# Two decoder layers on one core: order of the float32 products, of the readers of the column sums, of the sines, and one last store

## The chip, the cores and the metric

The kernel runs on one core of a Trainium2 chip. The metric is the device time of one execution in microseconds (us), lower is better. The time before is the median of three runs, 876.67 us (876.50 to 876.76).

## What is computed

A trunk of two layers on 256 tokens of width 1024, all in float32, then a last RMSNorm. The part that matters here is the first half of a layer:

```python
h = rmsnorm(x, norm_mix)
proj = h @ w_in                      # 8192 columns: cb, cc, cu, q, k, v, g, ga, gb
y_conv = short_conv_mixer(cb, cc, cu, conv_w, w_conv_out)
# retention: 4 heads, q and k rotated by cos/sin of the positions
scores = einsum(q, k) * decay        # 128 x 128 within a chunk; 2 chunks
o = scores @ v + what the state of the first chunk gives
o = (o - mean(o)) * rsqrt(var(o) + EPS) * ret_norm
y_ret = (silu(g) * o) @ w_ret_out
x = x + (sigmoid(ga) * y_conv + sigmoid(gb) * y_ret) @ w_o
x = x + square(relu(rmsnorm(x, norm_mlp) @ w_up)) @ w_down
```

`rmsnorm` and the norm of `o` are worked out as one over a square root of column sums; the sums come from products with a matrix of ones, so they stand in PSUM.

## The kernel before, in words

Every weight is cut into blocks of 1024 x 256 (512 KB in two halves); there are 152. `window(products)` (L153) is the unit of the program: one call per block. The call number `i` runs the work that `at(n, fn, ph=...)` (L132) had queued for it, in phases -1, 0, 1, 2, splits block `i + 2` between the phases, issues the products of block `i` on TensorE, and asks SP for block `i + 3`. The order on each engine is the order of these calls; no scheduler changes it.

To split (`split`, L104; `split_half`, L148) means that ACT casts a half block (128x1024) to a rounded part (L105) and DVE subtracts it from the half (L106), so that TensorE multiplies rounded and rest in `float32r`. `proj` (L183) multiplies one block: 16 pairs of a product with 512 columns and one with 256, the 256 one with the part that DVE made. The first pair of a block therefore waits for ACT, and its second product for DVE. After a block the sums in PSUM are collected: ACT copies one part (L234), DVE adds the other (L235).

The places that the change touches:

- `rsqrt_begin` (L244) reads column sums `v` from PSUM twice: ACT takes the root (L246), DVE the scaled mean plus EPS (L247). It is called from `factors_begin` (L408; first norm of each layer, 128x256, in window 6 of layer 0) and from `head_roots` (L582; twice per layer, 128x512, for the variances of two heads each; at 158 and 168 us in layer 0, 585 and 595 us in layer 1). The two Newton steps on the root (`newton`, L238) are in later windows: ACT squares (L240), DVE multiplies twice (L241, L242).
- `sines` (L388), in layer 0 alone: three ACT functions (L391 to L393) with a table of their own, at the end of window 5. `rotation_tables` (L395) on POOL makes `sin_t` and `cos_t` from them (L397 to L401) in window 6. `rotations` (L422, DVE, L424) uses them in window 8.
- `scores` (L541): per head three `float32r` products of 256 columns (`three`, L537), then one full float32 product of 128 columns (TensorE runs it as two records) for the second chunk. `mix_values` (L554): the same for the values, two groups per head, where the float32 product adds into half of the columns of the group.
- the end (L842 to L848): DVE scales the last 512 columns of the second 128 tokens in two pieces, SP stores each (L819); ACT scales and stores the other 512 columns.

Of the kernel before, what the change touches and what calls it, by code (L numbers as in the profile page):

```python
# [16 lines left out]
ALU = mybir.AluOpType  # L17

P = 128
D = 1024  # L20
T = 256
# [4 lines left out]
EPS = 1e-6  # L26
# [27 lines left out]
def trunk_kernel(ctx, tc, px, pos, w, mask, gf, out):  # L54
    nc = tc.nc
# [28 lines left out]
    def stile(name):  # L84
        return s8.tile([P, KT, T], F32, tag="s8", name=name)

    class Parts:
# [5 lines left out]
        def at(self, k):  # L93
            return self.tiles[k // (KT // 2)][:, k % (KT // 2)]
# [34 lines left out]
    work, small_products, amid = {}, {}, {}  # L129
# [50 lines left out]
    def mm(o, a, b, start, stop):  # L180
        nc.tensor.matmul(o, lhsT=a, rhs=b, start=start, stop=stop, skip_group_check=True)  # L181

    def proj(act, n_blocks=1):  # L183

        ps = ps_main.tile([P, 2, 2, T], F32, tag="mm", name="ps")

        def products(blk, b):  # L190
            for k in range(KT):
                a = act[b].at(k)
                for j in range(2):
                    first, end = b == 0 and k == 0, b == n_blocks - 1 and k == KT - 1
                    mm(ps[:, j], blk[:, 0, 2 * k + j, :], a, first, False)
                    mm(ps[:, j, 1], blk[:, 1, 2 * k + j, :], a[:, 0], False, end)
                    for fn, args in amid.pop((cnt[0], 2 * k + j), []):
                        fn(*args)

        for b in range(n_blocks):  # L200
            window(lambda blk: products(blk, b))
        return ps
# [40 lines left out]

    def rsqrt_begin(y, m, v, scale):  # L244

        nc.scalar.activation(y, v, AF.Abs_reciprocal_sqrt, scale=scale, bias=eps)  # L246
        nc.vector.tensor_scalar(out=m, in0=v, scalar1=scale, scalar2=EPS, op0=ALU.mult, op1=ALU.add)  # L247

    def column_sums(o, hi, lo):

# [87 lines left out]
    for n in range(2):  # L338
        c = slice(4 * n, 4 * n + 4)
# [9 lines left out]
    def first_parts(norm=norm):  # L349

        def parts(i, *ks):
            for n, k in enumerate(ks):
                norm.split(k)
                split_half(i, n)

        at(0, parts, 1, 2, 3)
        at(1, parts, 2, 4, 5)
        at(2, parts, 3, 6, 7)
        at(3, norm.split, 0)
        for i, half in ((4, 0), (4, 1)):  # L360
            at(3, split_half, i, half)
        for p in range(NPAIR):
            at(3 if p < 3 else 4, norm.square, p)
        at(4, norm.fold)
        at(5, norm.split_sum)
# [37 lines left out]
    for layer in range(DEPTH):  # L403
# [4 lines left out]
        def factors_begin(norm=norm):  # L408
            rs_m, rs_a = (tmp.tile([P, T], F32, tag="tmp1", bufs=7, name=n) for n in ("rs_m", "rs_a"))
            rsqrt_begin(rr, rs_m, norm.total_ps, 1.0 / D)  # L410
            at(1, newton, rr, rs_a, rs_m, ph=-1)
            at(2, factors_end, rs_m, rs_a, ph=-1)
# [17 lines left out]
        if layer == 0:  # L430
            first_parts()
            at(0, reduce_angles)
            at(5, sines, ph=2)
            at(6, rotation_tables)
            at(9, nc.sync.dma_start, mask_sb, mask)
        if layer == 0:
            products_at(5, norm_total)
# [5 lines left out]
        v1 = s4.tile([P, HEADS, T], F32, tag="s4", name="v1")  # L443
        qk = q_parts = k0_parts = sg = ta = tb = None
        yc, yr = None, Parts("yr", 0)
        sc0_parts = sc1 = None
# [87 lines left out]
            nc.gpsimd.tensor_tensor(out=acc, in0=y, in1=acc, op=ALU.mult)  # L534
            at(1, split, acc, *yc.pair(p))

        def three(o, a, b, stop):  # L537
            for n, (i, j) in enumerate(((0, 0), (0, 1), (1, 0))):
                mm(o, a[i], b[j], n == 0, stop and n == 2)

        def scores(h):  # L541
            ps = ps_misc.tile([P, T + P], F32, tag="misc", name="sc_ps")
            q, k = qk[:, h, P:], qk[:, HEADS + h, P:]
            three(ps[:, :T], [k0_parts[:, i, h, :] for i in range(2)], [q_parts[:, i, h, :] for i in range(2)], True)
            mm(ps[:, T:], k, q, True, True)
            at(1, weigh_scores, h, ps)

        def weigh_scores(h, ps):
# [5 lines left out]
        def mix_values(h):  # L554
            ps = ps_misc.tile([P, 2, T], F32, tag="misc", name="o_ps")
            for j in range(2):
                c = slice(j * P, (j + 1) * P)
                three(
                    ps[:, j, :], [v0_parts[:, i, h, c] for i in range(2)],
                    [sc0_parts[:, i, h, :] for i in range(2)], False,  # L560
                )
                mm(ps[:, j, P:], v1[:, h, c], sc1[:, h, :], False, True)
            at(1, gate_values, h, ps)

        def gate_values(h, ps):
# [16 lines left out]
        def head_roots(i, st):  # L582

            if i == 0:
                new("rm", s8.tile([P, 2, HEADS, T], F32, tag="s8", name="rm"))
            rm = kept["rm"]
            h = slice(2 * i, 2 * i + 2)
            rs = rm[:, 0, h, :]
            rsqrt_begin(rs, rm[:, 1, h, :], st, 1.0 / T)
            later = 2 + i  # L590
            for n in range(2):
                at(later + n, lambda: newton(rs, t2("rs_a"), rm[:, 1, h, :]))
            for n in range(2):
                at(later + 1 + n, head_out, 2 * i + n, rs[:, n, :])
# [17 lines left out]
        for name, _ in IN_ORDER:  # L612
            n = seen[name] = seen.get(name, -1) + 1
            if name == "q" and n == 0:
                qk = stile("qk")
                q_parts = s8.tile([P, 2, HEADS, T], F32R, tag="s8", name="q_parts")
                k0_parts = s4.tile([P, 2, HEADS, P], F32R, tag="s4", name="k0_parts")
            elif name == "cc" and n == 0:
                yc = Parts("yc")
            elif name == "cc" and n == 2:  # L620
                sc0_parts = s8.tile([P, 2, HEADS, T], F32R, tag="s8", name="sc0_parts")
                sc1 = s4.tile([P, HEADS, P], F32, tag="s2", bufs=1, name="sc1")
                for h in range(HEADS):
                    products_at(1 + h, scores, h)
            elif name == "g" and n == 2:
                osq = s8.tile([P, 2, HEADS, T], F32R, tag="s8", name="osq")
                for h, later in enumerate((0, 0, 1, 2)):
                    products_at(later, mix_values, h)
                products_at(2, head_sums, 0)
                products_at(4, head_sums, 1)  # L630
            elif name == "ga" and n == 0:
                ta = stile("ta")
            elif name == "gb" and n == 0:
                tb = stile("tb")
            ps = proj(act)
# [112 lines left out]
    o = stile("o").rearrange("p k t -> p (k t)")  # L748
    o = [o[:, j * D:(j + 1) * D] for j in range(2)]
# [9 lines left out]
    ps = [[both_ps[:, c] for c in HALVES], [third[:, HALVES[0]], ps_misc.tile([P, 512], F32, tag="misc", name="ps")]]  # L759
# [37 lines left out]
    def root(j):  # L797

        rest, part = sums[j][:, 0:1], sums[j][:, 1:2]
        m, r, a = (small.tile([P, 1], F32, tag=f"{n}{j}", bufs=1, name=n) for n in ("fin_m", "fin_r", "fin_a"))  # L800
        nc.scalar.activation(r, part, AF.Sqrt, bias=rest)
        nc.vector.tensor_tensor(out=m, in0=part, in1=rest, op=ALU.add)
        nc.vector.reciprocal(r, r)
        nc.vector.scalar_tensor_tensor(out=a, in0=r, scalar=m, in1=r, op0=ALU.mult, op1=ALU.mult)
        nc.vector.scalar_tensor_tensor(out=r, in0=a, scalar=3.0, in1=r, op0=ALU.subtract, op1=ALU.mult)
        return r
# [6 lines left out]
    def scaled(j, n, c, r):  # L813

        f = slice(512 * n + c.start, 512 * n + c.stop)
        nc.vector.scalar_tensor_tensor(
            out=o[j][:, f], in0=ps[j][n][:, c], scalar=r, in1=gain[:, f], op0=ALU.mult, op1=ALU.mult
        )
        nc.sync.dma_start(out=out[tok[j], f], in_=o[j][:, f])  # L819
# [19 lines left out]
    c = HALVES[0]  # L839
# [2 lines left out]
    nc.vector.tensor_tensor(out=o[1][:, c], in0=ps[1][0], in1=gain[:, c], op=ALU.mult)  # L842
    squares(1, 1)
    r = root(1)
    for n in range(2):
        scaled(1, 1, slice(256 * n, 256 * n + 256), r)
    nc.scalar.activation(o[1][:, c], o[1][:, c], AF.Copy, scale=r)
    nc.scalar.dma_start(out=out[tok[1], c], in_=o[1][:, c])  # L848

# [73 lines left out]
```

## Time and profile before

| | |
|---|---|
| median of 3 runs | 876.67 us |
| the profiled execution's own time | 876.84 us |
| its span | 875.0 us, 12663 instructions |
| TensorE products busy | 866.8 us, 99% |
| weight loads on TensorE busy | 754.1 us, 86% |
| DVE busy | 680.2 us, 78% |
| ACT busy | 529.5 us, 61% |
| POOL busy | 308.4 us, 35% |
| granted TensorE clock | full, 0.999 in the mean |
| HBM read | 161.66 MB, 186 GB/s |

The profile page gives the busy share of each engine and a chain of waits; the views of the trace give each instruction with its start, its length and, in brackets, how long its engine had been idle and what ended that. TensorE is busy nearly all the time, so the end moves only where TensorE waits, where its work gets longer or shorter, or behind its last product.

### The profile page before, as it was taken

What the parts mean: (1) busy time and instruction counts of PE and PEld (TensorE: products, weight loads), DVE (VectorE), ACT (ScalarE), POOL (GpSimd) and SP (SyncE); (2) the same over time, 40 slices, a digit from 0 to 9 for tenths busy, and PEclk for the clock granted to TensorE, in tenths of its full rate; (3) what the DMA queues carried; (4) which work ended last, traced back from release to release, by engine and by line L of the source; (5) the groups of instructions that cost most, each with busy time, mean ns of one, the idle gap of its engine ahead of it and who ended that gap; (6) DMA issues with size and microseconds to landing.
All of it is one profiled execution on the core that took longest, in us unless ns stands there. A gap on an engine that the chain in (4) does not pass through costs nothing.

```text
span 875.0 us, 12663 instructions
## 1 busy us (share of the span) xinstructions
PE 866.8 (99%) x4846; PEld 754.1 (86%) x4846; DVE 680.2 (78%) x739; ACT 529.5 (61%) x761; POOL 308.4 (35%) x191
## 2 busy tenths in 40 slices
PE   9999999999999999999999999999999999999997
PEld 6888888888888888888888888888888888888885
DVE  5799899999898766555567989999979896663443
ACT  6766665956467777444447665578645587772333
POOL 3857755361213222000013587455411322240000
PEclk9999999999999999999999999999999999999999
DMA  9746455556655655555554555545565565565541
GB/s 329 231 170 208 138 194 183 168 174 226 202 194 170 216 187 193 196 188 187 178 199 167 183 172 195 171 158 187 185 210 175 194 198 189 191 218 171 196 137 48
DMA packets 45996, 163.53 MB, mean 187 GB/s; under 512 B 5104, under 2 KB 5744, under 8 KB 45936
## 3 DMA queue, kind: packets, MB, share of 16 engines
q1 hardware_dynamic: 45648, 162.29, 55.4%
q8 instruction: 38, 0.62, 0.3%
q10 hardware_dynamic: 288, 0.44, 0.2%
q14 instruction: 22, 0.18, 0.1%
HBM read 161.66 MB, written 1.05 MB: 186 GB/s over the span
## 4 chain that ended last, share of the span: by engine, by line
PE 87%; POOL 5%; DVE 4%; DMA 1%; ACT 1%; issue 1%; SPq 0%; DVEq 0%; POOLq 0%
PE ps L181 85%; DVE parts L106 2%; PE o_ps L181 1%; DMA pos_i<-pos 1%; POOL red L371 1%; POOL ang L386 1%; DMA raw<-w 1%; POOL mix_sum L281 1%; POOL rot L458 1%; POOL qk L459 0%; DVE sum L235 0%; PE sc_ps L181 0%; ACT parts L105 0%; POOL qk L451 0%; POOL acc L534 0%
## 5 line engine op out<-in xcount | busy, mean ns | idle before, releaser
L106 DVE TENSOR_TENSOR parts<-raw,parts 128x1024 fp32r<-128x1024 f32 (+1 forms) x304 | 436.7, 1474 | 94.2 <-ACT parts L105 93.8
L105 ACT CAST parts<-raw 128x1024 fp32r<-128x1024 f32 (+1 forms) x304 | 304.5, 1049 | 110.8 <-PE ps L181 79.8
L181 PE MATMUL ps<-mix,parts 128*128 128x512 f32 (+1 forms) x1792 | 316.1, 337 | 1.0 <-DVE parts L106 1.0
L181 PEld LDWEIGHTS ps<-mix,parts 128*128 128x128 f32 x1792 | 274.0, 188 | 38.9 <-DVE parts L106 1.6
L181 PE MATMUL ps<-mlp,parts 128*128 128x512 f32 (+1 forms) x1024 | 178.1, 336 | 0.0
L181 PEld LDWEIGHTS ps<-mlp,parts 128*128 128x128 f32 x1024 | 156.5, 188 | 20.9
L730 POOL TENSOR_TENSOR u<-u,rr2m 128x512 f32<-128x512 f32 x32 | 46.5, 1454 | 126.2 <-ACT u L729 113.1
L235 DVE TENSOR_TENSOR sum<-ps,sum 128x512 f32<-128x512 f32 x78 | 53.3, 684 | 47.4 <-ACT sum L234 47.3
L181 PE MATMUL ps<-up,parts 128*128 128x512 f32 (+1 forms) x512 | 88.9, 336 | 0.0
L181 PE MATMUL ps<-parts,up 128*128 128x512 f32 x384 | 87.5, 389 | 0.0
L181 PEld LDWEIGHTS ps<-up,parts 128*128 128x128 f32 x512 | 78.3, 188 | 10.5
L181 PEld LDWEIGHTS ps<-parts,up 128*128 128x128 f32 x384 | 71.9, 188 | 14.9
L234 ACT COPY sum<-ps 128x512 f32<-128x512 f32 x78 | 45.4, 583 | 61.9 <-PE ps L181 61.7
L181 PE MATMUL ps<-yr,parts 128*128 128x512 f32 (+1 forms) x256 | 44.7, 336 | 0.0
L181 PE MATMUL ps<-mg,parts 128*128 128x512 f32 (+1 forms) x256 | 44.7, 336 | 0.0
L181 PE MATMUL ps<-yc,parts 128*128 128x512 f32 (+1 forms) x256 | 44.7, 336 | 0.0
L181 PEld LDWEIGHTS ps<-yc,parts 128*128 128x128 f32 x256 | 39.1, 188 | 5.2
L181 PEld LDWEIGHTS ps<-yr,parts 128*128 128x128 f32 x256 | 39.1, 188 | 5.2
L181 PEld LDWEIGHTS ps<-mg,parts 128*128 128x128 f32 x256 | 39.1, 188 | 5.2
L181 PE MATMUL ps<-parts,mix 128*128 128x512 f32 x180 | 41.6, 392 | 0.0
L181 PEld LDWEIGHTS ps<-parts,mix 128*128 128x128 f32 x180 | 33.7, 188 | 7.5 <-ACT parts L105 0.6
L281 POOL TENSOR_TENSOR mix_sum<-mix_sum,sq 128x512 f32<-128x512 f32 x6 | 9.9, 1644 | 83.4 <-ACT sq L279 83.2
(166 smaller groups left out, 747.5 us busy)
## 6 DMA issues: line engine op xcount, KB each, us to landing
raw<-w SPq DMA_DIRECT2D x302, 512.0 KB, 4.0
raw<-w SPq DMA_DIRECT2D x4, 256.0 KB, 5.0
px_sb<-px SPq DMA_DIRECT2D x3, 256.0 KB, 7.3
mask_sb<-mask SPq DMA_DIRECT2D x1, 512.0 KB, 7.6
gain<-gf SPq DMA_DIRECT2D x1, 512.0 KB, 4.5
out<-o SPq DMA_DIRECT2D x2, 256.0 KB, 2.1
out<-o SPq DMA_DIRECT2D x2, 128.0 KB, 2.0
out<-o ACTq DMA_DIRECT2D x1, 256.0 KB, 2.2
```

The lines of the kernel that those rows point to most:

```text
L105: nc.scalar.copy(hi, src)
L106: nc.vector.tensor_tensor(out=lo, in0=src, in1=hi.bitcast(F32), op=ALU.subtract)
L181: nc.tensor.matmul(o, lhsT=a, rhs=b, start=start, stop=stop, skip_group_check=True)
L234: nc.scalar.copy(t, ps[:, :, 1, :])
L235: nc.vector.tensor_tensor(out=t, in0=ps[:, :, 0, :], in1=t, op=ALU.add)
L281: nc.gpsimd.tensor_tensor(out=self.sum, in0=self.sum, in1=sq, op=ALU.add)
L371: nc.gpsimd.tensor_scalar(out=out, in0=x_, scalar1=c0, op0=ALU.mult, **ops)
L386: nc.gpsimd.tensor_tensor(out=ang, in0=ang, in1=red, op=ALU.subtract)
L458: nc.gpsimd.tensor_tensor(out=w_, in0=w_, in1=both(sinr), op=ALU.mult)
L730: nc.gpsimd.tensor_tensor(out=u, in0=u, in1=both(rr2), op=ALU.mult)
```

## The change

Four edits. The mean on DVE is written ahead of the root on ACT in `rsqrt_begin`; the sines and the rotation tables go one window later; the float32 product goes to the first place in `scores` and to the second in each group of `mix_values`; the last two pieces of the output become one piece and one store.

```diff
     def rsqrt_begin(y, m, v, scale):
 
+        nc.vector.tensor_scalar(out=m, in0=v, scalar1=scale, scalar2=EPS, op0=ALU.mult, op1=ALU.add)
         nc.scalar.activation(y, v, AF.Abs_reciprocal_sqrt, scale=scale, bias=eps)
-        nc.vector.tensor_scalar(out=m, in0=v, scalar1=scale, scalar2=EPS, op0=ALU.mult, op1=ALU.add)
...
             at(0, reduce_angles)
-            at(5, sines, ph=2)
-            at(6, rotation_tables)
+            at(6, sines, ph=2)
+            at(7, rotation_tables)
...
-        def three(o, a, b, stop):
+        def three(o, a, b, amid=lambda: None):
+
             for n, (i, j) in enumerate(((0, 0), (0, 1), (1, 0))):
-                mm(o, a[i], b[j], n == 0, stop and n == 2)
+                mm(o, a[i], b[j], n == 0, n == 2)
+                if n == 0:
+                    amid()
...
-            three(ps[:, :T], [k0_parts[:, i, h, :] for i in range(2)], [q_parts[:, i, h, :] for i in range(2)], True)
             mm(ps[:, T:], k, q, True, True)
+            three(ps[:, :T], [k0_parts[:, i, h, :] for i in range(2)], [q_parts[:, i, h, :] for i in range(2)])
...
-                    [sc0_parts[:, i, h, :] for i in range(2)], False,
+                    [sc0_parts[:, i, h, :] for i in range(2)],
+                    lambda: mm(ps[:, j, P:], v1[:, h, c], sc1[:, h, :], False, False),
                 )
-                mm(ps[:, j, P:], v1[:, h, c], sc1[:, h, :], False, True)
...
-    for n in range(2):
-        scaled(1, 1, slice(256 * n, 256 * n + 256), r)
+    scaled(1, 1, c, r)
```

On ACT, in windows 5 to 7 of layer 0, the piece of the difference (a + is the changed kernel; `rr` is the root, `mix_st` the column sums, `sh` and `turns` the sines, `parts` the halves of the weight blocks, `sg` a collected gate):

```order
 L105 CAST parts<-raw 128x1024
+L247 ACT_TABLE_LOAD
+L247 ACTIVATE rr<-mix_st,eps 128x256
+L481 ACTIVATE v_parts<-vt,mu 128x256 x2
+L234 COPY sg<-ps 128x512
+L105 CAST parts<-raw 128x1024 x2
 L391 ACT_TABLE_LOAD
 L391 ACTIVATE sh<-ang 128x256
 L392 ACTIVATE turns<-ang 128x256
 L393 ACTIVATE turns<-turns,quarter_turn 128x256
-L246 ACT_TABLE_LOAD
-L246 ACTIVATE rr<-mix_st,eps 128x256
```

The root and the two casts of window 6 now stand ahead of the sines; the number of table loads is the same.

At the first `head_roots` of layer 0, before: ACT (first four rows, `rm` is the root, `var_ps` the sums) and DVE (last four), with the semaphores that each row waits for:

```order
L567 ACTIVATE osq<-o_ps 128x512 [waits DVE_49,PE_49]
L246 ACT_TABLE_LOAD
L246 ACTIVATE rm<-var_ps,eps 128x512 [waits PE_49]
L234 COPY ta<-ps 128x512
...
L570 SCALAR_TENSOR_TENSOR sg<-o_ps,hg,sg 128x256
L247 TENSOR_SCALAR rm<-var_ps 128x512 [waits Activation_49]
L235 TENSOR_TENSOR ta<-ps,ta 128x512 [waits Activation_49]
L106 TENSOR_TENSOR parts<-raw,parts 128x1024 [waits DMAHW7_49,Activation_49]
```

The same place in the changed kernel:

```order
L570 ACTIVATE osq<-o_ps 128x512 [waits DVE_49,PE_49]
L247 ACT_TABLE_LOAD
L247 ACTIVATE rm<-var_ps,eps 128x512 [waits DVE_49]
L234 COPY ta<-ps 128x512
...
L573 SCALAR_TENSOR_TENSOR sg<-o_ps,hg,sg 128x256
L246 TENSOR_SCALAR rm<-var_ps 128x512 [waits PE_49]
L235 TENSOR_TENSOR ta<-ps,ta 128x512 [waits Activation_49]
L106 TENSOR_TENSOR parts<-raw,parts 128x1024 [waits DMAHW7_49,Activation_49]
```

No instruction changes its place on its engine here; the wait between the two readers of the sums turns round: before, DVE waits for ACT's root, now ACT's root waits for DVE.

## Rows read from the trace of the kernel before

**Rows 1.** Timeline of TensorE's weight loads: start us, us, engine, what [idle before <-releaser]
```profile
95.59 0.19 PEld L181 LDWEIGHTS ps<-mix,parts 128*128 128x128 f32 x1 [0.95 <-DVE parts L106]
...
107.89 0.19 PEld L181 LDWEIGHTS ps<-mix,parts 128*128 128x128 f32 x1 [0.66 <-DVE parts L106]
```

**Rows 2.** Busy time by window: window, its us, busy us of each engine, clock, DMA
```profile
46.50:78.80 32.30, 32.30 (x188) 28.49 (x187) 32.04 (x33) 20.43 (x30) 18.65 (x11) 1.00 0.57 194
...
156.50:214.90 58.40, 58.40 (x338) 51.46 (x338) 57.80 (x56) 42.58 (x57) 24.52 (x13) 1.00 0.58 190
```

**Rows 3.** Timeline of DVE around the first norm of layer 0
```profile
40.01 1.23 DVE L106 TENSOR_TENSOR parts<-raw,parts 128x1024 fp32r<-128x1024 f32 x1 [0.21 <-ACT parts L105]
44.38 0.42 DVE L247 TENSOR_SCALAR rs_m<-mix_st 128x256 f32<-128x256 f32 x1 [3.14 <-ACT rr L246]
...
46.59 2.58 DVE L106 TENSOR_TENSOR parts<-raw,parts 128x1024 fp32r<-128x1024 f32 x2 [0.19 <-ACT parts L105]
...
50.48 2.35 DVE L106 TENSOR_TENSOR parts<-raw,parts 128x1024 fp32r<-128x1024 f32 x2
52.74 0.42 DVE L241 SCALAR_TENSOR_TENSOR rs_a<-rs_a,rs_m 128x256 f32<-128x256 f32 x1
```

**Rows 4.** Timeline of ACT in the same stretch
```profile
39.99 1.28 ACT L391 ACT_TABLE_LOAD   x1
...
43.87 0.47 ACT L246 ACTIVATE rr<-mix_st,eps 128x256 f32<-128x256 f32 x1
...
47.41 0.41 ACT L240 ACTIVATE rs_a<-rr 128x256 f32<-128x256 f32 x1
```

**Rows 5.** Timeline of POOL, and of DVE beside it, in the same stretch
```profile
42.64 0.74 POOL L397 TENSOR_TENSOR sin_t<-sh,turns 128x256 f32<-128x256 f32 x1 [3.26 <-ACT turns L393]
...
44.37 0.61 POOL L400 TENSOR_TENSOR cos_t<-sh 128x256 f32<-128x256 f32 x1
...
46.58 1.96 POOL L482 TENSOR_SCALAR v<-vt,mu 128x256 f32<-128x256 f32 x1
...
47.75 1.41 DVE L106 TENSOR_TENSOR parts<-raw,parts 128x1024 fp32r<-128x1024 f32 x1
```

**Rows 6.** Timelines of ACT and DVE at the head roots of layer 0
```profile
158.05 0.69 ACT L246 ACTIVATE rm<-var_ps,eps 128x512 f32<-128x512 f32 x1
...
159.10 1.06 ACT L105 CAST parts<-raw 128x1024 fp32r<-128x1024 f32 x1
...
168.09 0.69 ACT L246 ACTIVATE rm<-var_ps,eps 128x512 f32<-128x512 f32 x1
...
159.06 0.68 DVE L247 TENSOR_SCALAR rm<-var_ps 128x512 f32<-128x512 f32 x1
...
160.26 1.21 DVE L106 TENSOR_TENSOR parts<-raw,parts 128x1024 fp32r<-128x1024 f32 x1
...
169.49 0.69 DVE L247 TENSOR_SCALAR rm<-var_ps 128x512 f32<-128x512 f32 x1
```

**Rows 7.** Timelines of DVE and TensorE at the third block of `yc`
```profile
199.98 1.21 DVE L106 TENSOR_TENSOR parts<-raw,parts 128x1024 fp32r<-128x1024 f32 x1
...
204.07 0.51 PE L181 MATMUL ps<-yc,parts 128*128 128x512 f32 x2
```

**Rows 8.** Chain of waits in order of time, layer 0: start us, us, what
```profile
113.48 0.57 PE sc_ps L181 x5
...
137.41 2.31 PE o_ps L181 x20
```

**Rows 9.** Timeline of the end, and the table of DMA issues (last number: us to landing)
```profile
870.88 0.88 DVE L816 SCALAR_TENSOR_TENSOR o<-ps,fin_r,gain 128x256 f32<-128x256 f32 x2
871.39 0.81 SPq L819 DMA_DIRECT2D out<-o  x2
871.63 0.35 ACTq L848 DMA_DIRECT2D out<-o  x1
...
out<-o ACTq DMA_DIRECT2D x1, 256.0 KB, 2.2
```

## The prediction

> **What bounds the kernel now.** I looked at the page's busy shares first: TensorE is at work 99% of the span at full clock. So a microsecond saved on DVE, ACT or POOL counts only if TensorE waited for it, and the reader should look for TensorE's waits next. After the first 10 us, which the change leaves alone, there are two, both in layer 0 and both for the part of a block that DVE makes: 0.95 and 0.66 us, 1.6 us together [rows 1]. They are the end of a backlog: from 46.5 to 78.8 us DVE is busy 32.04 of 32.30 us [rows 2], and behind that the chain goes over POOL, which DVE releases, to the same blocks. A second stretch matters where TensorE does not wait: from 156.5 to 214.9 us DVE is busy 57.80 of 58.40 us [rows 2], so whatever delays it there is not made up before 215 us. The tightest block in it is the third of `yc`: DVE ends its half at 199.98 + 1.21 = 201.19, TensorE starts the block at 204.07 and wants that half for its second product, some 0.2 us on [rows 7]. The reserve is about 3.1 us. Behind the last product there are only the last norm and the stores.
>
> **Float32 products: 0.** Nothing is added; 8 products for scores and 16 for values change places. A group of three `float32r` products and one float32 product takes 0.57 us in the scores, where a 512-column product follows, and 2.31 / 4 = 0.58 in the values, where mostly a 256-column product follows [rows 8]. What stands behind the float32 product thus makes 0.01 us. Every neighbour it gets is of a kind it had somewhere before (a 256-column product ahead, a 256- or 512-column one behind). Taking 0.01 us either way for 24 products bounds the edit at -0.2 to +0.2 us; I take 0. Its earlier wait for POOL or DVE is covered too: its operands are made ahead of the split parts that the other three products of its group need.
>
> **First norm of layer 0: the root, the sines, the tables.** Before, ACT ran the sines first, from 39.99, and the root began at 43.87 [rows 4]; DVE sat idle 3.14 us until then, because its mean waited for ACT's root [rows 3]. Now:
>
> - DVE takes the mean right behind the half that ends at 40.01 + 1.23 = 41.24, so it ends at 41.7. ACT has its table by 39.99 + 1.28 = 41.27 and must wait for the mean: the root starts at 41.7, 2.2 us earlier. The mean costs ACT 0.4 us here.
> - From root to first Newton square ACT took 47.41 - 43.87 = 3.54. Now the sines lie between: 43.87 - 39.99 less one load of 1.28, so 2.60. The square starts at 41.7 + 3.54 + 2.60 = 47.84 and ends at 48.25, 0.4 later than before.
> - DVE's two halves, which ended at 46.59 + 2.58 = 49.17 [rows 3], end 2.2 earlier, at 47.0. The Newton step behind them now waits for ACT's square until 48.25, 0.9 us ahead of the old 49.17. To the second Newton step at 52.74 it is 3.6 us of DVE's own work. Undisturbed, DVE is there at 51.85: 0.9 ahead.
> - It isn't undisturbed. The tables on POOL, from 42.64 on [rows 5], ran while DVE was idle. Now they start at 47.8, beside DVE's work. The first, 0.74, overlaps the first Newton step by some 0.3; the other two-input step, 0.61, falls on a half of a block, and I charge 0.25; the scalar steps I charge at 0.15, since a half beside such a step took 1.41 instead of 1.21 [rows 5, 7]. Together 0.7.
>
> So DVE comes 0.2 us earlier out of window 7, and TensorE's two waits shrink by 0.2 together. Between bounds of 0.9 (POOL costs nothing) and -0.3 (worked out under the third rival) I choose by those rows. The ceiling is the 1.6 us of waits.
>
> The Trainium skill, page "SBUF — State Buffer", section "Who interferes with whom", has a harder rule: a VectorE instruction with two inputs in SBUF and a GpSimd instruction that reads SBUF shut each other out for the whole instruction. By it this term would be a loss of 0.3 us, the lower bound above, instead of a gain of 0.2. The row here is milder: the half at 47.75 went on beside a scalar step that lasted until 48.54, and lost only 0.2.
>
> **Head roots, both layers: what the turned wait costs.** This is the edit's hidden price. In `head_roots` ACT used to be ahead: its root ran at 158.05, and DVE, deep in its queue, read the sums at 159.06 and had not waited. Now the root waits for the mean, until 159.06 + 0.68 = 159.74: ACT and everything behind it (the collecting copy, both casts) is 1.7 us later. DVE waits for these in turn. From root to the end of the first cast ACT takes 159.10 + 1.06 - 158.05 = 2.11, so DVE's next half can start 2.1 us behind the mean instead of 160.26 - 159.74 = 0.5 [rows 6]: 1.6 us lost. The second pair has the same order (168.09 against 169.49, [rows 6]), so it loses 1.6 again. DVE is 3.2 us late from 171 us on, against a reserve of 3.1: TensorE waits 0.1. Bounds: 0, if DVE makes something up, to 2.3, if POOL, released during DVE's waits, gets in ahead of a half at each pair, at 1.1 a time (what a second half loses beside POOL's 512-column steps is of the size of a half, 1.21). Layer 1 repeats it, but there nothing waits in the rows, and I charge 0. In the first norm of layer 1 DVE has no backlog, so the turned wait costs nothing.
>
> **Last store: -0.3.** Two pieces of 256 columns take DVE from 870.88 to 871.76, and SP issues the second store until 871.39 + 0.81 = 872.20. One piece of 512 columns out of PSUM should take about 0.7 (the 512-column mean in [rows 6] took 0.68), so the store is issued from 871.6, at the time of ACT's own (871.63), and lands at the same time [rows 9]. ACT's lands 2.2 later, at 873.8; the second piece's issue started near 871.8, at the end of a queue of three, and at 2.2 lands at 874.0 or a little later. Bounds 0 (the larger store takes longer by what it starts earlier) to -0.4; I take -0.3.
>
> **Sum.** 0 - 0.2 + 0.1 - 0.3 = -0.4 us on the profiled execution's 876.84, which stands 0.17 above the median of 876.67. On the median that is 876.3.
>
> **Rivals.**
>
> - Faster: POOL's tables cost DVE nothing and the two orders of POOL and DVE fall well, so that the chain comes 0.9 to 1.6 us early and TensorE's waits go. For it: ACT's new order frees 2.2 us. Against it: the Newton square itself is 0.4 late. With the store that is 876.67 - 0.9 - 0.3 = 875.5 down to 874.8. Chance 0.14.
> - Slower: the turned wait in `head_roots`. For it: DVE's full stretch [rows 2], which gives nothing back. It decides the time once DVE's delay passes 3.1 us; at 5.4 (2 x 1.6 and 2 x 1.1) TensorE waits 2.3 in layer 0, and the time is 876.67 + 2.3 - 0.3 = 878.7; at half of that, 877.5. Against it: the order of POOL and DVE has to fall badly twice. Chance 0.12.
> - Nothing: POOL's steps shut DVE out for their whole length. Then the second half of the Newton step waits out the whole scalar step of the tables, some 0.5 us more than charged, the front loses 0.3 and the store gains 0.3: 876.67 + 0.3 + 0.1 - 0.3 = 876.8. Chance 0.12. (This is the rule of the Trainium skill named above.)
>
> **How the numbers follow.** The forecast, 876.3, has the chance that is left, 0.62; its own bounds are about 875.4 to 877.2. The range goes to 875.1 on the faster side and to 877.5 on the slower, and leaves out the far half of either rival. About 0.2% of this time, 1.75 us, is what a measurement can tell from no change. Faster by more than that needs 874.9: only the far end of the first rival, 0.07. Slower needs 878.4: the far part of the second, 0.06. The rest, 0.87, is the same.
>
> **What would show it.** Right: on ACT the root of the first norm starts near 41.7 and the sines behind 45; DVE's idle time of 3.14 us is split into smaller ones, one of them ended by ACT's square; TensorE's two waits add up to 1.2 to 1.6 us. At the head roots ACT's root starts right behind DVE's mean, with idle time of 1.5 to 2 us on ACT and about 1.3 us on DVE ahead of its collecting add, twice per layer; the reserve at the third block of `yc` is near nothing. SP has one store at the end, near 871.6 on the old scale. The float32 groups stay at 0.57 to 0.58. Wrong: TensorE's waits gone, or new waits of over 0.5 us between 170 and 215 us, or float32 groups that differ by more than 0.02 us.

## The result, and the profile after

The changed kernel takes 882.11 us (median of 4 runs, 880.0 to 883.52) where the kernel before took 876.67 in the same session (876.5 to 876.76). The ratio is 1.0056, with a 95% interval of 1.0041 to 1.0072: 5 us **slower**, and far more scattered. The forecast was 876.3, with a range up to 877.5. The profiled execution took 881.02 us, 4.18 more than the profiled one before.

TensorE's waits do not explain it. These are its waits behind the first 10 us, by weight loads (engine, line, what for: us in total, times, longest), in the changed kernel:

```profile
PEld ps L181 <- DVE parts L106: 0.7, 2, 0.5
...
PEld var_ps L181 <- DVE osq L106: 0.2, 1, 0.2
```

The waits for `parts` went from 1.6 us [rows 1] to 0.7, and there is one new wait, of 0.2 us, for `osq`. That is less waiting than before, though the waits for `parts` are no measure of the change: in the profiles of the experiments below, they are none in four kernels, one of which has the old order of the first norm, and up to 1.7 us ahead of 110 us in the others. So the chain in order of time has to say where the time went. Before (start us, us, what, number of matmuls):

```profile
139.72 5.66 PE ps L181 x32
...
165.39 105.40 PE ps L181 x608
...
271.02 188.89 PE ps L181 x1060
...
700.79 168.37 PE ps L181 x864
```

After:

```profile
153.98 11.29 PE ps L181 x64
...
165.87 105.39 PE ps L181 x608
271.49 192.07 PE ps L181 x1060
...
704.51 168.37 PE ps L181 x864
```

One long row differs: the same 1060 matmuls, most of them the first MLP's, take 192.07 us instead of 188.89. TensorE neither waits in it nor does anything else; it only starts its matmuls at larger distances. The whole difference adds up: 0.48 at the start of the 608 matmuls (165.87 - 165.39; most of it from single blocks that are slower too, as at 153.98, where two blocks take 11.29 us), 3.18 in the MLP, some 0.06 in layer 1 (704.51 - 700.79 is 3.72), and 0.47 behind the last product, 4.2 together.

The busy time by window (window; its us; busy us and number of instructions of PE, PEld, DVE, ACT, POOL; granted clock; DMA share; GB/s) shows the same. Before:

```profile
94.00:166.00 72.00, 71.02 (x426) 62.53 (x425) 69.10 (x77) 45.46 (x68) 43.62 (x24) 1.00 0.53 173
...
280.00:440.00 160.00, 160.00 (x921) 140.90 (x920) 99.73 (x111) 91.58 (x124) 24.22 (x17) 1.00 0.57 193
```

After:

```profile
94.00:166.00 72.00, 71.87 (x427) 62.89 (x426) 69.55 (x76) 44.05 (x66) 39.67 (x23) 1.00 0.50 165
...
280.00:440.00 160.00, 160.00 (x907) 138.82 (x906) 97.93 (x105) 90.62 (x122) 23.82 (x17) 1.00 0.57 190
```

In the same 160 us TensorE starts 907 matmuls instead of 921, 1.5% fewer, at a granted clock of 1.00 (the 2.4 GHz level) in both. Between 94 and 166 us it is idle for 0.13 us instead of 0.98, and still gets through only one matmul more. A block of 32 matmuls (sixteen of 512 columns, each followed by one of 256) takes either 5.55 us or 5.65 us. **Both paces stand in the chain before**: the block at 139.72 took 5.66, while 105.40 / 608 x 32 = 5.55. The change moved some thirty blocks from one pace to the other.

Two things about this execution have to be kept in mind. TensorE has no wait at 271 us, where its long slow stretch begins; the row ahead of that is the two products of the MLP's column sums. And the one wait of TensorE behind 110 us, the one for `osq` at 165 us, is followed by the faster pace (105.39). So this profile by itself does not tie the slower pace to a wait; that rests on the experiments.

What is new in the waits is the one for `osq`. These rows run from the readers of the first heads' sums to the product of the second heads' sums. Timelines of ACT, DVE and TensorE's weight loads, before:

```profile
161.00 0.41 ACT L105 CAST osq<-osq 128x256 fp32r<-128x256 f32 x1
...
163.63 0.41 DVE L106 TENSOR_TENSOR osq<-osq 128x256 fp32r<-128x256 f32 x1
...
164.65 0.30 PEld L181 LDWEIGHTS var_ps<-osq,ones 128*128 128x128 f32 x2
```

After:

```profile
159.43 0.69 ACT L247 ACTIVATE rm<-var_ps,eps 128x512 f32<-128x512 f32 x1 [1.73 <-DVE rm L246]
...
162.38 0.41 ACT L105 CAST osq<-osq 128x256 fp32r<-128x256 f32 x1
...
158.72 0.68 DVE L246 TENSOR_SCALAR rm<-var_ps 128x512 f32<-128x512 f32 x1
160.63 0.69 DVE L235 TENSOR_TENSOR ta<-ps,ta 128x512 f32<-128x512 f32 x1 [1.23 <-ACT ta L234]
...
164.91 0.41 DVE L106 TENSOR_TENSOR osq<-osq 128x256 fp32r<-128x256 f32 x1
...
165.00 0.19 PEld L181 LDWEIGHTS var_ps<-osq,ones 128*128 128x128 f32 x1
165.37 0.19 PEld L181 LDWEIGHTS var_ps<-osq,ones 128*128 128x128 f32 x1 [0.18 <-DVE osq L106]
```

ACT's root waits 1.73 us for DVE's mean, as predicted. Everything behind it on ACT is late, the `osq` cast by 1.38 us (162.38 for 161.00), so DVE's `osq` step by 1.28. Before, that step ended at 163.63 + 0.41 = 164.04, and the second product of the sums began its load at 164.65 + 0.30 - 0.19 = 164.76: a reserve of 0.7 us. Now the step ends at 165.32, and TensorE waits.

The front, ACT, DVE and POOL after:

```profile
41.70 0.47 ACT L247 ACTIVATE rr<-mix_st,eps 128x256 f32<-128x256 f32 x1 [0.33 <-DVE rs_m L246]
...
45.36 1.28 ACT L391 ACT_TABLE_LOAD   x1
...
48.26 0.76 DVE L241 SCALAR_TENSOR_TENSOR rs_a<-rs_a,rs_m 128x256 f32<-128x256 f32 x1 [1.48 <-ACT rs_a L240]
...
52.75 0.41 DVE L241 SCALAR_TENSOR_TENSOR rs_a<-rs_a,rs_m 128x256 f32<-128x256 f32 x1
...
48.01 0.74 POOL L397 TENSOR_TENSOR sin_t<-sh,turns 128x256 f32<-128x256 f32 x1 [5.88 <-ACT turns L393]
```

The root begins at 41.70 where it was 43.87 [rows 4], the Newton square releases DVE at 48.26, and the second Newton step starts at 52.75 where it was 52.74 [rows 3]: nothing gained. And the end (DVE, ACT's queue, SP's queue, and the table of DMA issues):

```profile
874.59 0.75 DVE L819 SCALAR_TENSOR_TENSOR o<-ps,fin_r,gain 128x512 f32<-128x512 f32 x1
...
875.34 0.38 ACTq L850 DMA_DIRECT2D out<-o  x1
...
875.37 0.33 SPq L822 DMA_DIRECT2D out<-o  x1
...
out<-o ACTq DMA_DIRECT2D x1, 256.0 KB, 2.9
```

The last multiplication starts 881.02 - 874.59 = 6.43 us ahead of the end; before it was 876.84 - 870.88 = 5.96 [rows 9]. ACT's store takes 2.9 us to land where it took 2.2.

### The profile page after: what moved, and what is told of

Same layout as the page of the kernel before. It is cut to its first block, busy times and chain, and to the rows that moved or that the text cites. A ratio compares the mean times of both kernels' runs of the same rounds, so it can differ in the third digit from the quotient of the medians.

```text
span 879.2 us, 12653 instructions
## 1 busy us (share of the span) xinstructions
PE 871.8 (99%) x4846; PEld 754.7 (86%) x4846; DVE 681.3 (77%) x738; ACT 529.3 (60%) x761; POOL 303.3 (35%) x191
## 3 DMA queue, kind: packets, MB, share of 16 engines
HBM read 161.66 MB, written 1.05 MB: 185 GB/s over the span
## 4 chain that ended last, share of the span: by engine, by line
PE 87%; POOL 5%; DVE 4%; ACT 1%; DMA 1%; issue 1%; SPq 0%; POOLq 0%; DVEq 0%
PE ps L181 85%; DVE parts L106 2%; PE o_ps L181 1%; DMA pos_i<-pos 1%; POOL red L371 1%; POOL mix_sum L281 1%; POOL ang L386 1%; POOL rot L458 1%; POOL qk L459 0%; PE sc_ps L181 0%; ACT parts L105 0%; DMA px_sb<-px 0%; DVE sum L235 0%; POOL qk L451 0%; POOL sum L513 0%
```

## The experiments

Four theories were put down in the expectations. A: the place of the float32 products sets TensorE's pace. B: the exchange in `rsqrt_begin` does, by way of the later heads' sums. After the first four runs B became C: a wait of TensorE at those sums draws the slower pace, whatever makes the wait. D, against it: the exchanged order itself costs. Every kernel was timed beside the kernel before.

**One edit alone, or all but one.** The first kernel is the one before with the new `three`, `scores` and `mix_values` only. In `scores` that is:

```diff
-            three(ps[:, :T], [k0_parts[:, i, h, :] for i in range(2)], [q_parts[:, i, h, :] for i in range(2)], True)
             mm(ps[:, T:], k, q, True, True)
+            three(ps[:, :T], [k0_parts[:, i, h, :] for i in range(2)], [q_parts[:, i, h, :] for i in range(2)])
```

> The kernel before with only the order of the Float32 products changed (first in `scores`, second of each half in `mix_values`). Theory A (the place of the Float32 products sets the cadence at which TensorE starts the 512+256 column pairs of the blocks that follow, and the lost time is that cadence): 878 to 884 us, with the matmuls of the first MLP (about 271 to 460 us) at about 340 ns for the 512-column form where the kernel before has 336, and `ps <- up` above 90 us busy where it had 88.9. Theory B (the later heads' sums after the exchange of DVE's step and ACT's root set it): 876.5 to 876.9 us, like the kernel before, mean 336 ns.

Measured: 877.32 us (10 runs, 876.47 to 877.73) beside 877.13, ratio 1.0002 (0.9992 to 1.0011). The second is the change with this edit, and the one in `mix_values`, turned back:

> The changed kernel with the Float32 products back at the end of their groups; the exchange in `rsqrt_begin`, the sines a block on and the one store stay. Theory A: 876.0 to 876.6 us, the 512-column matmuls of the first MLP at 336 ns. Theory B: 880 to 883 us, at about 340 ns between 271 and 460 us.

Measured: 882.98 us, ratio 1.0049 (1.0026 to 1.0072); the seven times are 877.0, 877.9, 881.0, 883.0, 883.1, 883.2 and 883.5. The wait and the slow rows of its profiled execution (882.98 us), weight loads and chain:

```profile
165.35 0.19 PEld L181 LDWEIGHTS var_ps<-osq,ones 128*128 128x128 f32 x1 [0.87 <-DVE osq L106]
...
165.85 107.41 PE ps L181 x608
...
273.49 192.08 PE ps L181 x1060
```

Here the slow pace begins right behind the wait, and costs 2.01 + 3.19 = 5.2 us. The third is the change without the exchange:

```diff
-        nc.vector.tensor_scalar(out=m, in0=v, scalar1=scale, scalar2=EPS, op0=ALU.mult, op1=ALU.add)
         nc.scalar.activation(y, v, AF.Abs_reciprocal_sqrt, scale=scale, bias=eps)
+        nc.vector.tensor_scalar(out=m, in0=v, scalar1=scale, scalar2=EPS, op0=ALU.mult, op1=ALU.add)
```

> The changed kernel with the exchange in `rsqrt_begin` undone. Theory A: as the changed kernel, 878 to 884 us. Theory B: 876.2 to 876.6 us, and the 0.2 us wait of the second heads' sums at about 165 us gone.

Measured: 877.16 us (10 runs, 876.04 to 877.68), ratio 0.9999 (0.999 to 1.0009). The fourth is the kernel before with that exchange and nothing else:

> The kernel before with only the exchange in `rsqrt_begin`. Theory A: 876.4 to 876.9 us. Theory B: 880 to 883 us, with the wait for `osq` at about 165 us and 340 ns for the 512-column matmuls of the first MLP. If both theories are wrong and the cadence falls out by chance in each execution, the single times of all four kernels spread over 2 us or more.

Measured: 879.38 us, ratio 1.0041 (1.0022 to 1.0059); the seven times run from 876.4 to 883.0. A has fallen: the two kernels with the exchange are slow and scattered, the two without it are neither, whatever the float32 products do. B holds, but not in every execution, so the median stays under the 880 us that it asked for. (The two kernels without the exchange are some 0.5 us above what B gave them; the kernel before itself took 877.13 beside them.) The profiled one of the fourth kernel took 876.36 us and has no wait at the sums (DVE, and the weight loads):

```profile
157.10 0.68 DVE L246 TENSOR_SCALAR rm<-var_ps 128x512 f32<-128x512 f32 x1
...
163.29 0.41 DVE L106 TENSOR_TENSOR osq<-osq 128x256 fp32r<-128x256 f32 x1
...
164.18 0.30 PEld L181 LDWEIGHTS var_ps<-osq,ones 128*128 128x128 f32 x2
```

DVE took the mean at 157.10 there, 1.6 us earlier than in the changed kernel, and `osq` was ready 0.6 us early. So whether TensorE waits at all seems to hang on where DVE's backlog of the front left it in that execution; only this one execution of the kernel has a profile, so the slow ones are not shown to have waited.

The first and third kernels also price the store, since both end without any late work ahead of it. Their last multiplications (two pieces of 256 in the first, one of 512 in the third):

```profile
870.51 0.88 DVE L819 SCALAR_TENSOR_TENSOR o<-ps,fin_r,gain 128x256 f32<-128x256 f32 x2
```

```profile
870.55 0.75 DVE L819 SCALAR_TENSOR_TENSOR o<-ps,fin_r,gain 128x512 f32<-128x512 f32 x1
```

To the end it is 876.47 - 870.51 = 5.96 us with two pieces, and 876.99 - 870.55 = 6.44 with one: the larger store costs 0.5 us. ACT's store lands after 2.2 us in each of the eight profiles that end with two pieces, and after 2.7 to 2.9 in each of the six that end with one. In the times of whole runs 0.5 us is too little to tell: the first and the third kernel differ by 0.2 us the other way.

**The wait without the exchange.** Two kernels with the same added work, told apart by its place only (`spare` is a tile of 128x256 that nothing reads):

```diff
+            if h == HEADS - 1:
+                for _ in range(4):
+                    at(1, nc.vector.tensor_tensor, spare, mask_sb[:, 0, :], mask_sb[:, 0, :], ALU.mult)
             at(1, split, sq[:, 0, :], osq[:, 0, h, :], osq[:, 1, h, :])
```

> The kernel before, with four DVE products of 128x256 values, which nothing reads, put right ahead of the last head's `osq` step (about 1.5 us). Theory C (a wait of TensorE for that step at the second heads' sums, 0.95 us away in the kernel before, draws the slower cadence for the blocks behind it): a wait of 0.3 to 0.8 us at about 165 us, then the 512-column matmuls at about 340 ns up to the next break of the stream, 879 to 883 us, single times spread over several us. Rival D (the exchange itself, the order in which DVE and ACT read the sums, is what costs): 876.8 to 877.6 us, the wait and no more.

In the other kernel the three lines stand behind the `split`:

> The same four products right behind the `osq` step. Theory C: no wait at the second heads' sums, 876.9 to 877.5 us, 336 ns. Rival D: the same. If the later work of DVE (the reserve of 3 us behind 170 us) is what counts, 878 us or more here too.

Measured: ahead, 882.97 us (882.63 to 883.68), ratio 1.0072 (1.0057 to 1.0087); behind, 877.2 us (876.21 to 877.84), ratio 1.0004 (0.9995 to 1.0013). Weight loads and chain with the work ahead:

```profile
165.84 0.19 PEld L182 LDWEIGHTS var_ps<-osq,ones 128*128 128x128 f32 x1 [0.97 <-DVE osq L107]
...
166.34 107.42 PE ps L182 x608
273.99 192.08 PE ps L182 x1060
```

Chain with the work behind:

```profile
165.72 105.40 PE ps L182 x608
271.35 188.89 PE ps L182 x1060
```

This shows that a wait is enough, and that the exchanged order is not needed for the loss. ACT and DVE read the sums in the old order in both, they do the same work, and the kernel that makes TensorE wait loses 6.0 us (882.97 beside 876.95). Of it, 2.02 + 3.19 = 5.2 are the slower pace; what is left is of the size of the wait. The wait is a little longer than expected, and the four times do not spread.

**The exchange without the wait.** Two ways to keep it out of TensorE's path, in the changed kernel. One gives `rsqrt_begin` a flag, so that `head_roots` has its old order and the norms the new one:

```diff
+        if root_first:
+            nc.scalar.activation(y, v, AF.Abs_reciprocal_sqrt, scale=scale, bias=eps)
         nc.vector.tensor_scalar(out=m, in0=v, scalar1=scale, scalar2=EPS, op0=ALU.mult, op1=ALU.add)
-        nc.scalar.activation(y, v, AF.Abs_reciprocal_sqrt, scale=scale, bias=eps)
+        if not root_first:
+            nc.scalar.activation(y, v, AF.Abs_reciprocal_sqrt, scale=scale, bias=eps)
...
-            rsqrt_begin(rs, rm[:, 1, h, :], st, 1.0 / T)
+            rsqrt_begin(rs, rm[:, 1, h, :], st, 1.0 / T, True)
```

> The changed kernel, with the exchange kept for the norm's sums and undone for the heads' sums. Theory C: 876.8 to 877.3 us, no spread. Rival D, with the norms' sums as the place that counts: 880 to 883 us, as the changed kernel.

The other has the second heads' sums a block later:

```diff
-                products_at(4, head_sums, 1)
+                products_at(5, head_sums, 1)
```

> The changed kernel as it is, the second heads' sums one block later (so their operand has some 5.5 us more). Theory C: 876.5 to 877.5 us, no wait for `osq`, unless a later reader of these sums' roots is late. Rival D: 880 to 883 us.

Measured: 877.62 us (875.81 to 878.08), ratio 1.0008 (0.9999 to 1.0018), and 877.62 us (877.12 to 878.55), ratio 1.0007 (0.9998 to 1.0017). Either one takes away the loss, as C says, and the profiled executions have no wait for `osq` and no long slow stretch (the second: 99.84 us for the 576 matmuls behind the sums and 188.89 for the 1060). The second keeps the exchanged order at the heads, so D falls: that order costs little where TensorE does not wait for it. Both medians lie a little above what was expected of C (877.3 and 877.5 at most); 0.5 us of that could be the one store, which both keep. Neither beats the kernel before.

**Another wait, a break, and another order of widths.** In the next kernel the three lines stand behind the `split`, with `range(12)` and for layer 0 only:

> The kernel before, with twelve of the products that nothing reads right behind the last head's `osq` step of layer 0 (about 4.8 us of DVE, where its reserve over the next blocks is 3.1 to 4.0 us): TensorE now waits for a plain block's weights, not at the sums, by some 0.8 to 1.7 us in all. If any wait draws the slower cadence: 881 to 884 us, the matmuls behind the wait at about 340 ns as far as 460 us. If it takes the wait between the two products of the column sums: 877.5 to 879 us, the wait alone, 336 ns.

Measured: 881.54 us (881.19 to 881.72), ratio 1.0049 (1.0034 to 1.0064). Weight loads and chain:

```profile
178.63 16.66 PEld L182 LDWEIGHTS ps<-mix,parts 128*128 128x128 f32 x95 [1.85 <-DVE parts L107]
...
178.64 96.13 PE ps L182 x543
275.01 188.90 PE ps L182 x1060
```

A wait for a plain block's weights draws the slower pace too: 543 matmuls at 105.40 / 608 each would take 94.1 us, and took 96.1. But this time the pace went back at the MLP's column sums, where in the kernels above that were slow behind the heads' sums it stayed. So both expectations were half right: the wait need not be at the sums, and how long the pace holds is not settled by the wait. In the kernel with the wait at the sums, a break was put in behind the third block of the MLP:

```diff
+        def kick(a=norm.act.at(0)):
+            spare_ps = ps_misc.tile([P, 2 * T], F32, tag="misc", name="spare_ps")
+            for n in range(4):
+                mm(spare_ps, ones, a.rearrange("p s t -> p (s t)"), True, True)
+
+        if layer == 0:
+            products_at(2, kick)
```

> The kernel with four products ahead of the `osq` step (882.97 us), and four Float32r products of 512 columns, which nothing reads, behind the third block of the first MLP. If the cadence is a phase that a stretch of other matmuls resets: the slow stretch ends at about 283 us, 2.9 us saved and 0.9 us spent, 880.5 to 881.5 us. If it holds on whatever comes between, or has another cause (data, memory): 883.5 to 884.0 us.

Measured: 883.01 us (880.87 to 883.87), ratio 1.0062 (1.0047 to 1.0077). This decides nothing. In the profiled execution, of 880.87 us, the pace had gone back ahead of the break:

```profile
274.08 5.55 PE ps L182 x32
...
280.56 183.35 PE ps L182 x1028
```

and of the other three times (882.7, 883.3 and 883.9 us) two lie between the two expectations and one on the second.

Read together, the chains show more. In the old order of widths the 608 matmuls take 105.4 or 107.4 us and the 1060 take 188.9 or 192.1, and nothing between, unless the stretch is broken on the way. Within a stretch of blocks the pace holds; it changes where the stretch is broken, by a group of other products (scores, values, column sums) or by a wait of TensorE. Which pace follows a break is not fixed by the break. Up to 160 us this last kernel does the same work in the same order as the kernel before, and TensorE waited for the same half by nearly the same time, 0.64 us for 0.66 [rows 1]. Weight loads here:

```profile
108.03 5.36 PEld L182 LDWEIGHTS ps<-mix,parts 128*128 128x128 f32 x31 [0.64 <-DVE parts L107]
...
126.49 11.25 PEld L182 LDWEIGHTS ps<-mix,parts 128*128 128x128 f32 x64
```

And in the kernel before:

```profile
126.04 11.05 PEld L181 LDWEIGHTS ps<-mix,parts 128*128 128x128 f32 x64
```

Here the blocks behind that wait go at the slower pace, there at the faster. So a wait can bring the slower pace; it does not always do so. Where TensorE never waits the pattern repeats: in layer 1 every profile with the same order of products has its slow blocks at the same places, and only those. A wait may thus change the pace behind later breaks as well, and the slow MLP of the changed kernel would fit that; no run shows it.

The last two kernels change the order in which `proj` issues its matmuls, in the kernel before and in the changed one:

```diff
                 for j in range(2):
                     mm(ps[:, j], blk[:, 0, 2 * k + j, :], a, first, False)
+                for j in range(2):
                     mm(ps[:, j, 1], blk[:, 1, 2 * k + j, :], a[:, 0], False, end)
```

> The kernel before, with the four matmuls of a step of `proj` in the order 512, 512, 256, 256 columns where it was 512, 256, 512, 256. Alone, 512-column products follow each other every 227 ns and 256-column ones every 112 to 121 ns in this kernel's rows; the pair took 346.7 ns or 353.3 ns. If the overhead hangs on the change of widths: about 340 to 343 ns for a pair, 865 to 873 us. If it hangs on the number of weight loads: no change, 876 to 878 us. Without the pairing of a hi and a lo part a slower cadence still may come: up to 890 us.

> The changed kernel with the same order of the four matmuls. If the two cadences belong to the alternation of 512 and 256 columns, the wait at the second heads' sums costs its own length here (0.2 to 0.6 us) and the time is within 1 us of the kernel before in the same order; if not, 4 to 6 us above it.

Measured: 879.31 us (10 runs, 879.0 to 879.79), ratio 1.0026 (1.0016 to 1.0035), and 880.43 us (880.36 to 880.74), ratio 1.0036 (1.0023 to 1.0049). Chain of the first, then weight loads and chain of the second:

```profile
165.19 105.90 PE ps L181 x608
271.32 189.67 PE ps L181 x1060
```

```profile
165.84 0.19 PEld L181 LDWEIGHTS var_ps<-osq,ones 128*128 128x128 f32 x1 [1.05 <-DVE osq L106]
...
166.34 105.91 PE ps L181 x608
272.48 189.67 PE ps L181 x1060
```

With 512, 512, 256, 256 columns there is one pace, a little slower (5.57 us a block), on either side of a wait of 1.05 us, and the single times of each kernel agree within 0.8 us. The change then costs 880.43 - 879.31 = 1.1 us in the medians, just over the 1 us that was expected and far from 4 to 6. Between the two profiled executions it is 1.5 us: 1.05 up to the last product, about the wait's own length, and 0.4 for the one store. So the long slow stretch was seen only with the order 512, 256, 512, 256. The hoped-for gain from fewer changes of width did not come. No version tried beats the kernel before.

## Why the prediction was wrong

- **Float32 products, 0: right within its bounds.** Alone they make 1.0002 (0.9992 to 1.0011), and the groups of scores take 0.57 to 0.58 us as foretold. The working left out that the new order has one block more per layer at the slower pace behind the groups (three for two in layer 1, where TensorE does not wait); that is the 0.06 us of layer 1. Theory A, that they set the pace, was mine after the result, and the first run refuted it.
- **First norm, -0.2: within its bounds, near nothing.** The root, the sines and the square stand where the working put them (41.7, behind 45, 48.26 for 48.25), but the tables on POOL and the first Newton step took what was gained by 52.75. Of the rule of the Trainium skill (page "SBUF — State Buffer", section "Who interferes with whom") the rows say this much: the Newton step that began at 48.26 took 0.76 us for the 0.41 of the same step at 52.75, beside POOL's two-input step, which lasted until 48.75. It lost 0.35 of the 0.49 us in which the two overlapped, about what was charged and less than the whole that the rule asks; the loss of 0.3 us worked out by the rule did not come, and neither did the gain of 0.2. That TensorE's waits in the front went from 1.6 to 0.7 us, where 1.2 to 1.6 were foretold, says nothing for or against the working: the first kernel of the experiments, which does not have this edit, shows none.
- **Head roots, +0.1: this step failed, twice.** The mechanism on ACT and DVE was right: the root's wait of 1.73 us against 1.7 foretold, and DVE's half at the third block of `yc`, which ended at 201.19, ends 2.8 us later against 3.2 foretold, and no wait came up there:

```profile
202.81 1.21 DVE L106 TENSOR_TENSOR parts<-raw,parts 128x1024 fp32r<-128x1024 f32 x1
```

  The first fault was the *place*. I looked for the smallest reserve among the halves of the weight blocks only, and found 3.1 us. TensorE also waits for `osq`, an operand of the sums, made on ACT and DVE behind the very root that was held up. Its reserve was 0.7 us, and a delay of 1.3 was enough. The second fault, the larger, was the *price*: a wait was charged at its own length. With the right place that would have been 1.3 - 0.7 = 0.6 us in place of 0.1, and a forecast of 876.8, inside the range. Shown is up to ten times that: 0.2 to 1.0 us of waiting, and with it up to 5.2 us of slower pace, which held to the next break or beyond it, at most to the first column sums of layer 1. That this term carries the loss is shown by the kernels that leave it out (the third, and the two of "The exchange without the wait"): none of them loses. By which way the wait of 0.18 us in the profiled execution led to the slow MLP, 106 us later, is not shown.
- **Last store, -0.3: wrong in sign, +0.5.** The start was right (874.59 + 0.75, and both stores are issued within 0.03 us). What the working left out is that two stores of 256 KB now run at the same time: ACT's, which ends last, lands 2.9 us after its issue instead of 2.2.
- **The rivals.** The slower one named the right edit, at the wrong place and price. My sign of a wrong prediction, new waits of over 0.5 us between 170 and 215 us, could not have caught it: the one new wait was of 0.2 us, at 165.

The data for a better forecast stood in the chain before: blocks of equal work at 5.55 and at 5.65 us, with no wait in them. A bound worked out from those two, over the 608 and 1060 matmuls behind the heads' sums, would have put 5 us on the slower side.

Left open: what fixes the pace behind a break of the stream. All four profiled executions with a wait at the second heads' sums in the old order of widths have a long slow stretch, but where it begins and ends differs: at the sums and up to the first column sums of layer 1 in two, at the sums and up to the MLP's column sums in one, and in the changed kernel only from the MLP's column sums on.

## What to carry to other kernels

Where an engine's wait is turned round, follow everything behind it on that engine to every operand that TensorE reads, small ones too, and compare the delay with the smallest of those reserves. Where equal blocks show two durations at one clock in the trace, a short wait may cost more than its length: take as the upper bound the difference of the two over all that follows, past the next change of work too, since the pace may or may not go back there. Two large stores issued at the same moment at the end can land later than one large and two small.

## What the runs showed of the hardware

- A stream that alternates 512- and 256-column matmuls, each with its own weights, has two paces at a granted clock of 1.00: 105.40 and 107.42 us for the same 608 matmuls, which is 346.7 and 353.4 ns for a pair. In these chains the pace changed only where other products or a wait of TensorE broke the stream. In the order 512, 256, 512, 256, the slower pace followed the waits of 0.42, 0.87, 0.97 and 1.85 us behind 160 us at once, and held for 96 to 300 us; behind a wait of 0.18 us the faster pace went on. Without any wait the slower pace is there for single blocks behind groups of other products (5.66 us at 139.72 in the kernel before), and for the 1060 matmuls from 271.49 us on in the changed kernel.
- The order 512, 512, 256, 256 showed one pace, 348.4 ns for two matmuls (105.90 / 304), with and without such a wait.
- A store of 256 KB landed 2.2 us after its issue beside two stores of 128 KB on the other queue, and 2.7 to 2.9 us beside one of 256 KB (issued 0.03 us later in the changed kernel).
